# A gated delta net's preparation and recurrence emitted with a scheduling priority 300 places over the projection beside them

## The chip, the core and the metric

The kernel runs on one core of a Trainium2 chip. Its engines are named as in the profile: PE is TensorE (PEld is its loading of weights), DVE is VectorE, ACT is ScalarE, POOL is GpSimd and SP is SyncE, which here only issues DMAs. Each engine works through a queue of its own in order, and waits at an instruction whose inputs or buffers another engine has not yet finished. The metric is the device time of one execution in microseconds; the kernel before takes 3442.72 us, the median of 3 runs (3442.59 to 3445.05).

## The reference

A streaming encoder of four layers: gated delta net, mLSTM, gated delta net, mLSTM, each followed by a convolutional feed-forward layer, over 16 learned tokens and 1024 frames of 1024 features. DEPTH is 2, so the kernel has one delta net and one mLSTM. Only the delta net is touched by the change. Its reference, cut to what matters (16 value heads, 8 query and key heads, head size 128):

```python
proj = h @ w_in
qkv = silu(causal_depthwise_conv(proj[..., :o1], conv_w))     # 4 taps
z = proj[..., o1:o2]                                          # the gate of the output
beta = sigmoid(proj[..., o2:o3])
g = -exp(a_log) * softplus(proj[..., o3:] + dt_bias)
q, k = l2_normalize(q), l2_normalize(k)                       # one q, k for two value heads
G = cumsum(g within a chunk)
decay = exp(G_i - G_j) where i >= j else 0
a_mat = eye + (k*beta) @ k.T * decay * strictly_lower
u, w = triangular_solve(a_mat, [v*beta, k*beta*exp(G)])
attn = q @ k.T * decay;  qd = q * exp(G);  kt = k * exp(G_last - G)
# over the chunks, state S:
v_new = u - w @ S
o = qd @ S + attn @ v_new
S = S * exp(G_last) + kt.T @ v_new
out = (rms_norm(o, norm_w) * silu(z)) @ w_out
```

## The kernel before

The 1044 used positions (16 + 1024, and four of padding) are cut into 3 blocks of 348, and the delta net works in chunks of 116, so three chunks to a block. Features lie across the 128 partitions. One query and key head with its two value heads, in one block, is a step n: 8 heads times 3 blocks are 24 steps, and head h has the steps 3h to 3h + 2. The profile shows the stage of these steps from 82.9 us to about 1140 us.

**The projection** of a head is six tiles of 128 features (`gi`): q, k, two of v and two gate tiles. A tile and a block are 24 matmuls of 128x348 into one PSUM bank `pj_gi` (L233 to L235, because a float32 product is made of three products of a rounded part `wh`, `xh` and a rest `wl`, `xl`). L308 (`take`) then reads the bank on DVE; for q, k and v the four convolution taps follow (one on ACT at L695, three on DVE at L697). The weights come by DMA into 9 raw buffers; ACT casts them (L137) and POOL subtracts (L138) into 10 split buffers, a tile ahead. While the delta net works on head h, the second half of its own gates and the first four tiles of head h + 1 are projected, two tiles beside each step. After the two tiles, **the silu burst** runs on ACT over their six pages (L724): a table load, six activations and a load of the table with exp and ln (L727). It already has a priority of 100000 and the order within it is fixed.

**The preparation** of a step (`gdn_prepare`) normalises k, computes the masked products kk and qk of k and q in each chunk (L576, L579), and then does for each of the two value heads (`decay_block`, then the first part of `inverse`): three transposes spread the decay over a bank `row` (L559); ACT makes `eG` of it (L561); DVE makes `E` (L566), and ACT its exponential (L567); DVE multiplies kk by E into `ah` and masks it to `l` (L911, L912); POOL makes `A` from the same (L914), its rest `al`, and the products `att` (L764) and `qd` (L767). eG, E and A share three buffers:

```python
eG = self.core.tile([P, BS], F32, tag="e", name=f"eG_{name}", bufs=3)   # L560
E = self.core.tile([CH, BS], F32, tag="e", name=f"E_{name}", bufs=3)    # L562
A = self.core.tile([CH, BS], F32, tag="e", name=f"A_{name}", bufs=3)    # L913
```

so that the second head's E has to wait until one of the first head's is no longer read. Then the triangular matrix is inverted (`inverse`): Z is l plus the identity (L920, DVE), the first matmul transposes it (L923), and six levels follow, each with three matmuls in turn (L949, L958 and a third) and an operation of DVE or ACT behind each (`pl` at L953, `X`, `Z`), all in float16; a correction step ends it. The inverses of the two value heads are advanced in turn. The matmuls of the projection fill TensorE's time while such a chain waits for DVE and ACT.

**The recurrence** of a step (`gdn_recur`) goes through three chunks: transposes of k and v (`tr`, L795; `vt` on ACT, `ktb` on DVE at L797), the product with the state (`ks`, L828), the solution (`w`, `wv`), the state's update (`S` at L848; `St` on DVE at L854, two a chunk), and the outputs. **The finish** (`gdn_finish`) normalises and gates the output of the step before (L262, L265 are the square root's ln and exp; `osq`, `gy`) and stores it.

**What sets the order.** Python generators are emitted in turn by `weave`, in proportion to the numbers beside them: in a step n the preparation of n + 1 (27 parts), the recurrence of n (14), the finish of n - 1 (4) and the projection (8), or for the last three steps the output projection (28). Every instruction gets a place by this order of emission. A scheduler then writes each engine's queue: among the instructions of an engine whose inputs its own timing model holds ready, the one with the smallest place goes next. `tc.high_priority(n)` makes it count as n places earlier. That is in use already at three places: the readers of PSUM banks (`take`, `combine`) and the accumulators have 300, and the silu burst 100000. PSUM has two banks each for the projection (`pj`), for all products of the preparation, recurrence and finish (`sp`), and for the inverse (`pp`, `px`).

Of the kernel before, what the change touches and what calls it, by code (L numbers as in the profile page):

```python
# [64 lines left out]
def weave(*parts):  # L65

    live = [[g, max(n, 1), 0] for g, n in parts]
    while live:
        p = min(live, key=lambda p: (p[2] + 0.5) / p[1])
        try:  # L70
            next(p[0])
            p[2] += 1
        except StopIteration:
            live.remove(p)


def run(g):
    for _ in g:
        pass


class Trunk:
# [185 lines left out]
    def over_features(self, ps, acc, name):  # L268

        nc = self.nc  # L270
        hi, lo = [self.page("part", f"{z}_{name}", 2, F32R)[:, : acc.shape[1]] for z in ("ah", "al")]
        nc.scalar.copy(hi, acc)
        nc.vector.tensor_tensor(lo, acc, hi.bitcast(F32), ALU.subtract)
        nc.tensor.matmul(ps, self.ones, hi, start=True, stop=False)
        nc.tensor.matmul(ps, self.ones, lo, start=False, stop=True)

    def const(self, v):
        return self.consts[v]
# [327 lines left out]
    def gdn(self):  # L606
        a = self.a
        self.o_dram = [self.pd.tile([P, 2, TP], F32, tag=f"o_g_{h}", name=f"o_g_{h}", bufs=1) for h in range(NQK)]
        self.pages_of = {}
        self.blocks = {}  # L610
        n_all = NQK * NB
        tiles = lambda h: [h, NQK + h, 2 * NQK + 2 * h, 2 * NQK + 2 * h + 1, 32 + 2 * h, 32 + 2 * h + 1]

        def silu(h, tiles):
            self.burst([y for i in tiles for y in self.pages_of[h, i]], self.last, AF.Silu)

        def project(n):


            h, part = divmod(n, NB)  # L620
            i = (4, 0, 2)[part]
            g = h + (part > 0)
            yield from self.gdn_project(g, tiles(g)[i : i + 2], i)
            silu(g, (i, i + 1))

        def enter(b):
            hs = []
            for m in range(KD):
                h = self.page("C", f"hs_in_{b}_{m}", N_PAGES)
                sl = slice(b * BS, (b + 1) * BS)  # L630
                nc.sync.dma_start(h, self.hs[:, m, sl])
                self.put_input(h, m, sl)
                hs.append(h)
            return hs

        nc = self.nc
        t0 = tiles(0)
        weights = lambda t: self.split_weights(a["gdn_w_in"][t], f"gi{t}")
        self.new_input(0, "in")
        self.rt = self.new_factors("in")  # L640
        wg = self.split_weights(a["gdn_gate_w"], "gdn_gates", 32)
        hs = [enter(0)]
        ws = [weights(t0[0])]
        self.tables()
        hs.append(enter(1))
        ws.append(weights(t0[1]))
        hs.append(enter(2))
        rows = []
        for b in range(NB):
            acc = self.squares(hs[b], f"in{b}")  # L650
            self.now.append(lambda acc=acc, b=b: self.norm(acc, f"in{b}", self.r(b)))
            rows.append(self.gate_rows(wg, b, "gdn"))
            if b == NB - 1:
                gates = self.gdn_gates(rows)
                next(gates)
            for i in range(2):
                run(self.gdn_unit(0, i, t0[i], ws[i], b))
        lb, tb = next(gates)
        silu(0, (0, 1))
        order = t0[2:4] + [t for h in range(NQK) for t in tiles(h)[4:] + (tiles(h + 1)[:4] if h + 1 < NQK else [])]  # L660
        self.queue_weights([(a["gdn_w_in"][t], f"gi{t}") for t in order], 1)

        def first():
            yield from self.gdn_project(0, tiles(0)[2:4], 2)
            silu(0, (2, 3))

        weave((self.gdn_prepare(0, tb, lb), 13), (first(), 6))
        out = self.out_projection(a["gdn_w_out"], NQK, "go", GDN_CORE, GDN_LATE, 1, 2)
        for n in range(n_all):
            parts = [(self.gdn_recur(n, tb), 14)]  # L670
            if n + 1 < n_all:
                parts.insert(0, (self.gdn_prepare(n + 1, tb, lb), 27))
            if n:
                parts.append((self.gdn_finish(n - 1), 4))
            parts.append((project(n), 8) if n <= n_all - NB else (islice(out, 28), 28))
            weave(*parts)
        weave((self.gdn_finish(n_all - 1), 4), (out, 30))
# [620 lines left out]
    def ffn(self, L, order, row, post, pre):  # L1298
# [19 lines left out]
        for t, g in seq:  # L1318
            run(group(t, g))
            if (t, g) == (1, 1) and pre is not None:  # L1320
                self.new_input(pre, name)
                for part in [z for p in self.xt for z in p]:
                    nc.gpsimd.memset(part[:, NTOK:].bitcast(F32), 0.0)
                for m in range(KD):
                    h = self.raw_input(f"hi_{name}_{m}").rearrange("p n c -> p (n c)")
                    nc.sync.dma_start(h, self.new_hs[:, m, :HB])
                    self.put_input(h, m, slice(0, HB))
# [54 lines left out]
    def ffn_phase(self, L, row, post, pre):  # L1382
        self.wide = True
        self.ffn_constants(L)
        order = self.ffn_plan(L)
        run(self.out)
        self.ffn(L, order, row, post, pre)
# [110 lines left out]
```

## Time and profile before

| | us |
|---|---|
| median of 3 runs | 3442.72 |
| the profiled execution | 3444.23 |
| its span in the trace | 3442.5 |
| up to the first prepared block (0 to 82.9) | 82.9 |
| the steps of the delta net (82.9 to 1113.4) | 1030.5 |
| the last blocks and the start of the output projection (1113.4 to 1240) | 126.6 |
| the rest: feed-forward and mLSTM layers (1240 to 3442.5) | 2202.5 |

Instructions stand in the profile with the line, the operation, the tile they write and those they read, their shape, how often (x), and behind the bar the busy time, the mean of one in ns, and the idle time of the engine before them. An item of the timeline has its start in us, its duration, and in brackets how long its engine waited ahead of it and for what. A row of the waits has the total in us, the count and the longest. Matmuls are pipelined, so that their durations overlap, and the start of the next one tells more than the end. The granted clock is 0.969 on average. The projection's matmuls are the largest group of the delta net on TensorE; the first of its three products:

```profile
L233 PE MATMUL pj_gi<-xh_in,wh_gi 128*128 128x348 f32 x1152 | 394.2, 342 | 5.5 <-ACT wh_gi L137 3.7
```

### The profile page before, as it was taken

The page shows a single profiled execution, that of the slowest core. Times are in us where ns is not written, and L with a number is a line of the kernel's source. Part 1 is how long each engine was busy: PE and PEld are TensorE (multiplying, and loading weights), DVE is VectorE, ACT ScalarE, POOL GpSimd, SP SyncE. Part 2 cuts the span into 40 slices and gives each one's busy share as a digit, 9 for nine tenths or more (in the row PEclk, how much of TensorE's full clock was granted, in tenths as well). Part 3 has the DMA queues.
Part 4 walks back from the last instruction along what each step waited for, and adds up shares of the span by engine and source line. Part 5 has one row for each costly group of instructions (what it writes and reads, how often), then busy time and mean ns, then how long its engine had stood idle before and what let it go on. Part 6 is the DMA issues. An engine that isn't in the chain of part 4 may idle for free. (4 is left out here: it accounts for less than half of the span.)

```text
span 3442.5 us, 68429 instructions
## 1 busy us (share of the span) xinstructions
PE 3212.2 (93%) x25368; PEld 3119.6 (91%) x25368; DVE 2373.1 (69%) x5143; ACT 1609.0 (47%) x3390; POOL 1652.2 (48%) x1890
## 2 busy tenths in 40 slices
PE   7999999999999998799999989899998799999998
PEld 6889988988988897799999989899998799999998
DVE  7777777777767649877677484534469867777474
ACT  5455545555545435655455243323345645445232
POOL 2433443444334444577665434333344477666453
PEclk9999999999999999899999999999999899999999
DMA  3011100101001344422224453211125422224452
GB/s 118 23 37 34 34 29 31 34 32 34 31 31 40 107 132 152 134 93 93 78 78 133 133 182 125 93 44 50 56 78 183 136 90 87 87 75 132 132 180 88
DMA packets 234511, 297.75 MB, mean 86 GB/s; under 512 B 20684, under 2 KB 167104, under 8 KB 234176
## 3 DMA queue, kind: packets, MB, share of 16 engines
q1 hardware_dynamic: 234176, 293.37, 26.3%
q8 instruction: 200, 3.28, 0.4%
q14 instruction: 135, 1.11, 0.1%
HBM read 240.06 MB, written 53.23 MB: 85 GB/s over the span
## 5 line engine op out<-in xcount | busy, mean ns | idle before, releaser
L233 PE MATMUL pj_gi<-xh_in,wh_gi 128*128 128x348 f32 x1152 | 394.2, 342 | 5.5 <-ACT wh_gi L137 3.7
L233 PE MATMUL dn_f<-so_f,wh_f 128*128 128x260 f32 x1344 | 386.6, 288 | 11.8 <-ACT wh_f L137 5.0
L235 PE MATMUL pj_gi<-xh_in,wl_gi 128*128 128x348 f32 x1152 | 395.7, 343 | 0.9 <-POOL wl_gi L138 0.9
L234 PE MATMUL pj_gi<-xl_in,wh_gi 128*128 128x348 f32 x1152 | 393.5, 342 | 0.0
L235 PE MATMUL dn_f<-so_f,wl_f 128*128 128x260 f32 x1344 | 384.7, 286 | 0.0
L234 PE MATMUL dn_f<-so_f,wh_f 128*128 128x260 f32 x1344 | 384.5, 286 | 0.0
L138 POOL TENSOR_TENSOR wl_f<-wr_f,wh_f 128x512 fp32r<-128x512 f32 x168 | 226.0, 1362 | 246.0 <-ACT wh_f L137 113.5
L1278 DVE SCALAR_TENSOR_TENSOR z<-u,fcw,z 128x260 f32<-128x260 f32 x528 | 243.4, 487 | 49.8 <-ACT z L1276 35.0
L138 POOL TENSOR_TENSOR wl_u_s<-wr_u,wh_u_s 128x512 fp32r<-128x512 f32 x176 | 228.2, 1300 | 97.7 <-ACT wh_u_s L137 97.3
L233 PEld LDWEIGHTS dn_f<-so_f,wh_f 128*128 128x128 f32 x1344 | 257.7, 192 | 13.6 <-ACT z L1276 5.5
L441 DVE TENSOR_TENSOR acc_f<-acc_f,dn_f 128x260 f32<-128x260 f32 x320 | 133.1, 421 | 189.2 <-PE dn_f L235 188.2
L234 PEld LDWEIGHTS dn_f<-so_f,wh_f 128*128 128x128 f32 x1344 | 258.2, 192 | 0.2
L235 PEld LDWEIGHTS dn_f<-so_f,wl_f 128*128 128x128 f32 x1344 | 258.2, 192 | 0.1
L1276 ACT ACTIVATE z<-u,fcb,fcw 128x260 f32<-128x260 f32 x352 | 192.3, 570 | 93.7 <-DVE u L196 92.4
L233 PEld LDWEIGHTS pj_gi<-xh_in,wh_gi 128*128 128x128 f32 x1152 | 222.1, 193 | 8.0 <-ACT wh_gi L137 4.0
L235 PEld LDWEIGHTS pj_gi<-xh_in,wl_gi 128*128 128x128 f32 x1152 | 222.6, 193 | 2.4 <-POOL wl_gi L138 1.2
L234 PEld LDWEIGHTS pj_gi<-xl_in,wh_gi 128*128 128x128 f32 x1152 | 222.2, 193 | 0.7 <-issue 0.2
L138 POOL TENSOR_TENSOR wl_gi<-wr_gi,wh_gi 128x512 fp32r<-128x512 f32 x96 | 132.4, 1380 | 157.8 <-ACT wh_gi L137 153.8
L137 ACT CAST wh_u_s<-wr_u 128x512 fp32r<-128x512 f32 x176 | 105.9, 615 | 192.5 <-PE up L234 134.9
L697 DVE SCALAR_TENSOR_TENSOR gy<-u_g,c_gdn_conv_w_g,gy 128x348 f32<-128x348 f32 x288 | 187.9, 663 | 7.9 <-ACT gy L695 5.4
L138 POOL TENSOR_TENSOR wl_u_a<-wr_u,wh_u_a 128x512 fp32r<-128x512 f32 x132 | 170.1, 1293 | 37.0 <-ACT wh_u_a L137 36.3
L137 ACT CAST wh_f<-wr_f 128x512 fp32r<-128x512 f32 x168 | 103.1, 617 | 178.8 <-PE dn_f L234 133.0
(501 smaller groups left out, 11718.0 us busy)
## 6 DMA issues: line engine op xcount, KB each, us to landing
wr_u<-in_ffn_w_up_dram SPq DMA_DIRECT2D x224, 256.0 KB, 2.6
wr_f<-in_ffn_w_down_dram SPq DMA_DIRECT2D x176, 256.0 KB, 2.8
wr_gi<-in_gdn_w_in_dram SPq DMA_DIRECT2D x96, 256.0 KB, 2.6
h<-y SPq DMA_DIRECT2D x176, 130.0 KB, 2.3
si_f<-h SPq DMA_DIRECT2D x88, 260.0 KB, 3.5
wr_go<-in_gdn_w_out_dram SPq DMA_DIRECT2D x64, 256.0 KB, 2.7
wr_mi<-in_ml_w_in_dram SPq DMA_DIRECT2D x44, 256.0 KB, 2.6
o_g<-gy SPq DMA_DIRECT2D x48, 174.0 KB, 1.8
```

Source lines behind the costliest of these rows:

```text
L137: nc.scalar.copy(hi, part(raw))
L138: nc.gpsimd.tensor_tensor(lo, part(raw), hi.bitcast(F32), ALU.subtract)
L233: nc.tensor.matmul(out, w[0], x[0], start=start, stop=False)
L234: nc.tensor.matmul(out, w[0], x[1], start=False, stop=False)
L235: nc.tensor.matmul(out, w[1], x[0], start=False, stop=stop)
L441: nc.vector.tensor_tensor(acc[m][n], acc[m][n], ps, ALU.add)
L697: ins = nc.vector.scalar_tensor_tensor(y, u[:, j : j + BS], taps[:, j : j + 1], y, ALU.mult, ALU.add)
L1276: nc.scalar.activation(z, p[:, 2 : 2 + QB], AF.Identity, scale=taps[:, 2:3], bias=self.fcb[:, tt : tt + 1])
L1278: nc.vector.scalar_tensor_tensor(z if i or not h else y[h], p[:, i : i + QB], taps[:, i : i + 1], z, ALU.mult, ALU.add)
```

## The change

The steps of `gdn_recur` and `gdn_prepare` in the loop over n are each emitted within `high_priority(300)`, and so count as 300 places earlier than the projection and the finish that are emitted beside them. The preparation of the first step, ahead of the loop, is as it was.

```diff
+CHAIN = 300
 
+    def in_front(self, g):
+
+        while True:
+            with self.tc.high_priority(CHAIN):
+                if next(g, g) is g:
+                    return
+            yield
 
         for n in range(n_all):
-            parts = [(self.gdn_recur(n, tb), 14)]
+            parts = [(self.in_front(self.gdn_recur(n, tb)), 14)]
             if n + 1 < n_all:
-                parts.insert(0, (self.gdn_prepare(n + 1, tb, lb), 27))
+                parts.insert(0, (self.in_front(self.gdn_prepare(n + 1, tb, lb)), 27))
             if n:
                 parts.append((self.gdn_finish(n - 1), 4))
             parts.append((project(n), 8) if n <= n_all - NB else (islice(out, 28), 28))
             weave(*parts)
```

The instructions are the same; their order in the queues of PE, DVE and ACT changes from the first steps of the delta net up to the end of its last block, and is the same before and behind. The changed file has four more lines ahead of the class and eight more from `in_front` on, so that a line such as L559 is L571 in it, and L234 is L238.

In DVE's queue, at the entrance of the inverse in block 0 of a head (the head of 619.9 to 756.3 us), before; `l_8_0` and `l_9_0` are the masked matrices (the buffers of `l0`) of the block's two value heads, `E_0_8398` the second head's E:

```order
L566 TENSOR_SCALAR E_0_8398<-row_0_8392,dt_s_gdn,gd_lb 116x116 x3
L797 TENSOR_TENSOR ktb_2_1_8420<-tr_2_1_8422,dt_kt_gdn 116x256
L920 TENSOR_TENSOR Z_0_8451<-l_8_0_8382,i_162 116x348
L911 TENSOR_TENSOR ah_0_8403<-scs_kk_0_8327,E_0_8398 116x348
L308 TENSOR_TENSOR u_g_0_8863<-pj_gi_0_8779,r_in 128x348
L912 TENSOR_TENSOR l_9_0_8405<-ah_0_8403,c_m_g 116x348
L953 TENSOR_TENSOR pl_0_2_8470<-pp_0_2_8466,c_mlev_g 116x174
L920 TENSOR_TENSOR Z_0_8459<-l_9_0_8405,i_162 116x348
```

And after:

```order
L578 TENSOR_SCALAR E_0_8398<-row_0_8392,dt_s_gdn,gd_lb 116x116 x3
L809 TENSOR_TENSOR ktb_2_1_8420<-tr_2_1_8422,dt_kt_gdn 116x256
L924 TENSOR_TENSOR l_8_0_8382<-ah_0_8380,c_m_g 116x348
L923 TENSOR_TENSOR ah_0_8403<-scs_kk_0_8327,E_0_8398 116x348
L932 TENSOR_TENSOR Z_0_8451<-l_8_0_8382,i_162 116x348
L924 TENSOR_TENSOR l_9_0_8405<-ah_0_8403,c_m_g 116x348
L866 SCALAR_TENSOR_TENSOR St_2_0_8481<-St_1_2_8080,dt_gt_gdn,S_2_0_8478 128x128 x2
L932 TENSOR_TENSOR Z_0_8459<-l_9_0_8405,i_162 116x348
```

The first head's mask `l_8_0` has moved from ahead of the second E to behind it, Z has moved from ahead of the second head's `ah` to behind it, and the projection's `u_g` has left this place.

In TensorE's queue, in block 2 of the same head, before; `pj_gi_1_9763` is a bank of the next projection, and the last matmul of the gate projection's bank `pj_gi_2_9536` stands 48 instructions ahead of the first of these rows:

```order
L576 MATMUL sc_kk_2_9592<-gy_2_8286 116x116 x3
L576 MATMUL sc_qk_2_9623<-gy_2_8059,gy_2_8286 116x116 x3
L233 MATMUL pj_gi_1_9763<-xh_in_105,wh_gi_1_9408 128x348
L828 MATMUL ks_1_0_9629<-St_0_2_9335,gy_1_8251 116x256
L234 MATMUL pj_gi_1_9763<-xl_in_106,wh_gi_1_9408 128x348
L235 MATMUL pj_gi_1_9763<-xh_in_105,wl_gi_1_9409 128x348
L233 MATMUL pj_gi_1_9763<-xh_in_107,wh_gi_1_9408 128x348
L559 MATMUL row_2_9638<-c_ident_g,dt_G_gdn 128x116 x3
```

And after, from the last two matmuls of the gate projection on:

```order
L238 MATMUL pj_gi_2_9536<-xl_in_108,wh_gi_1_8995 128x348
L239 MATMUL pj_gi_2_9536<-xh_in_107,wl_gi_1_8996 128x348
L237 MATMUL pj_gi_0_9610<-xh_in_93,wh_gi_0_9404 128x348
L238 MATMUL pj_gi_0_9610<-xl_in_94,wh_gi_0_9404 128x348
L588 MATMUL sc_kk_2_9592<-gy_2_8286 116x116 x3
L588 MATMUL sc_qk_2_9623<-gy_2_8059,gy_2_8286 116x116 x3
L239 MATMUL pj_gi_0_9610<-xh_in_93,wl_gi_0_9405 128x348
L840 MATMUL ks_1_0_9629<-St_0_2_9335,gy_1_8251 116x256
L237 MATMUL pj_gi_0_9610<-xh_in_95,wh_gi_0_9404 128x348
L571 MATMUL row_2_9638<-c_ident_g,dt_G_gdn 128x116 x3
```

Between the gate projection's last matmul and `row` stood 46 of the next projection's matmuls; now four stand there, and kk, qk and `row` follow the gate projection closely.

In ACT's queue at the same place, before; `rs_k` is of the preparation's norm, `gy_2_9561` the last page of the silu burst over the gate projection, and `eG_2_9642` reads the `row_2_9638` of the rows above:

```order
L724 ACTIVATE gy_2_9561<-gy_2_9561 128x348
L727 ACT_TABLE_LOAD
L262 ACTIVATE rs_k_2_9579<-kn_2_9572,cvals 128x348
L796 COPY vt_1_0_9585<-tr_1_0_9586 116x256
L265 ACTIVATE rs_k_2_9579<-rs_k_2_9579 128x348
L695 ACTIVATE gy_0_9709<-u_g_0_9710,c_gdn_conv_w_g 128x348
L272 CAST ah_o_0_9803<-osq_0_0_9635 128x348
L561 ACTIVATE eG_2_9642<-row_2_9638 128x348
L695 ACTIVATE gy_1_9859<-u_g_1_9860,c_gdn_conv_w_g 128x348
L567 ACTIVATE E_2_9644<-E_2_9644 116x348
```

And after:

```order
L736 ACTIVATE gy_1_9534<-gy_1_9534 128x348
L736 ACTIVATE gy_2_9561<-gy_2_9561 128x348
L739 ACT_TABLE_LOAD
L573 ACTIVATE eG_2_9642<-row_2_9638 128x348
L579 ACTIVATE E_2_9644<-E_2_9644 116x348
L573 ACTIVATE eG_2_9665<-row_2_9661 128x348
L707 ACTIVATE gy_0_9709<-u_g_0_9710,c_gdn_conv_w_g 128x348
```

The norm's two operations and the copy `vt` have moved ahead of the burst, and eG now stands directly behind the burst's second table load.

## The prediction

> **What bounds the kernel now.** I read the page first, then the busy times by stretch, then the waits of TensorE in one head.
>
> ```profile
> PE 3212.2 (93%) x25368; PEld 3119.6 (91%) x25368; DVE 2373.1 (69%) x5143; ACT 1609.0 (47%) x3390; POOL 1652.2 (48%) x1890
> ```
> ```profile
> 82.90:1113.40 1030.50, 968.52 (x8086) 922.45 (x8086) 774.65 (x1849) 525.59 (x1181) 409.86 (x500) 0.98 0.10 32
> 619.90:756.30 136.40, 128.65 (x1081) 122.47 (x1081) 103.56 (x248) 71.06 (x160) 54.97 (x69) 0.99 0.10 32
> ```
>
> The columns of the two stretches are length, then busy time of PE, PEld, DVE, ACT and POOL, granted clock, DMA share and GB/s. The first is the delta net from its first prepared block to its last projection: TensorE idles 62.0 us of 1030.5, and DMA is no limit (0.10). The second is one head, three blocks: 136.4 us, 7.75 of them idle. So TensorE is the bound, and the most that a better order could win here is about 62 us, 1.8% of the kernel. The heads repeat, so I work on this one head (blocks 0, 1 and 2) and multiply by 8. TensorE's two largest waits there of four (total us, count, longest), and two of the three kinds of matmul that make up the inverse's levels, over the first 1240 us:
>
> ```profile
> PE px L923 <- DVE Z L920: 5.6, 5, 1.5
> PE S L848 <- DVE E L566: 1.5, 2, 0.9
> ...
> ```
> ```profile
> L949 PE MATMUL pp<-X,ah 116*116 116x64 f16 (+2 forms) x864 | 91.8, 217 | 0.0
> L958 PE MATMUL px<-pl,Z 116*116 116x64 f16 (+2 forms) x864 | 88.2, 212 | 0.0
> ```
>
> The reader sees that 7.1 of the 7.75 us are lost at the entrance of the inverse: at its first matmul (L923, which needs Z) and at the state matmul beside it. The levels that follow (L949, L958) show 0.0 of idle time before them in the whole stage. **So this change is decided at the entrance.** There the chain in block 0 is:
>
> ```profile
> 625.76 0.51 PE L559 MATMUL row<-c_ident_g,dt_G_gdn 116*128 116x116 f32 x3 [0.23 <-DVE scs_qk L579]
> 626.31 0.46 ACT L561 ACTIVATE eG<-row 128x348 f32<-128x348 f32 x1 [1.11 <-PE row L559]
> 628.42 1.61 POOL L914 TENSOR_TENSOR A<-scs_kk,E 116x348 f32<-116x348 f32 x1 [0.64 <-ACT E L567]
> 629.99 1.03 POOL L764 TENSOR_TENSOR att<-scs_qk,E 116x348 f32<-116x348 f32 x1
> 631.05 1.01 DVE L566 TENSOR_SCALAR E<-row,dt_s_gdn,gd_lb 116x116 f32<-116x116 f32 x3 [0.83 <-POOL att L764]
> 631.98 0.41 DVE L797 TENSOR_TENSOR ktb<-tr,dt_kt_gdn 116x256 f32<-116x256 f32 x1
> 632.32 0.63 DVE L920 TENSOR_TENSOR Z<-l,i 116x348 f16<-116x348 f16 x1
> 632.86 1.25 DVE L911 TENSOR_TENSOR ah<-scs_kk,E 116x348 f16<-116x348 f32 x1
> 634.04 0.51 DVE L308 TENSOR_TENSOR u_g<-pj_gi,r_in 128x348 f32<-128x348 f32 x1
> 634.47 0.65 DVE L912 TENSOR_TENSOR l<-ah,c_m_g 116x348 f16<-116x348 f16 x1
> 635.03 0.33 DVE L953 TENSOR_TENSOR pl<-pp,c_mlev_g 116x174 f16<-116x174 f32 x1
> 635.28 0.73 DVE L920 TENSOR_TENSOR Z<-l,i 116x348 f16<-116x348 f16 x1
> 635.93 0.59 DVE L854 SCALAR_TENSOR_TENSOR St<-St,dt_gt_gdn,S 128x128 f32<-128x128 f32 x2
> 636.07 0.37 PE L923 MATMUL px<-i,Z 116*116 116x116 f16 x3 [0.99 <-DVE Z L920]
> ```
>
> From the row matmul to the second inverse's L923 are 10.31 us. The second E comes 5.29 us after the row matmul; 2.6 of them are GpSimd's A and att, which give its buffer back only when att ends (631.02). A scheduling priority changes none of these durations, only how many projection matmuls lie beside them and what stands ahead of them in a queue. Blocks 1 and 2, from row to second L923:
>
> ```profile
> 669.54 0.51 PE L559 MATMUL row<-c_ident_g,dt_G_gdn 116*128 116x116 f32 x3
> 680.01 0.37 PE L923 MATMUL px<-i,Z 116*116 116x116 f16 x3 [0.49 <-DVE Z L920]
> 709.71 0.46 PE L559 MATMUL row<-c_ident_g,dt_G_gdn 116*128 116x116 f32 x3
> 721.51 0.37 PE L923 MATMUL px<-i,Z 116*116 116x116 f16 x3 [1.24 <-DVE Z L920]
> ```
>
> That is 10.47 and 11.80 us.
>
> **Term 1: the filler at the entrance.** The price of a projection matmul:
>
> ```profile
> 622.89 0.87 PE L576 MATMUL sc_kk<-gy 128*116 128x116 f32 x6
> 624.13 0.41 PE L234 MATMUL pj_gi<-xl_in,wh_gi 128*128 128x348 f32 x1
> 624.38 0.69 PE L828 MATMUL ks<-St,gy 128*116 128x256 f32 x2
> 624.71 0.51 PE L235 MATMUL pj_gi<-xh_in,wl_gi 128*128 128x348 f32 x1
> 625.06 0.32 PE L233 MATMUL pj_gi<-xh_in,wh_gi 128*128 128x348 f32 x1
> 625.21 0.32 PE L234 MATMUL pj_gi<-xl_in,wh_gi 128*128 128x348 f32 x1
> ```
>
> Durations overlap, so starts count: 0.15 to 0.16 us for a projection matmul behind another (625.06 to 625.21), 0.25 behind a chain matmul (624.13 to 624.38), so a change from chain to projection costs about 0.09. Between the row matmul and the second L923 the order has 35, 33 and 37 projection and finish matmuls now, and 30, 29 and 47 after the change. With 0.16 each, six or seven changes (0.5), and the chain's own matmuls there (about 1.6 to 2.2 us), the filler is 7.8, 8.1 and 8.0 us now, and 7.4, 7.2 and 10.1 then. What the chain needs beyond its filler is stall: now 2.5 + 2.3 + 3.8 = 8.6 us a head (the wait view shows a little less, since it counts from modelled ends).
>
> **Term 2: DVE's queue at the entrance.** Block 0's queue after the second E becomes ktb, l, ah, Z, l, two St, Z, where it was ktb, Z, ah, u_g, l, pl, Z. By start-to-start times: 0.34 + 0.56 + 1.18 + 0.54 + 0.56 + 0.59 + 0.65 = 4.42 against 3.95 us (the St pair by its 0.59). The first l moved from the shadow of the wait at 631.05 to behind it. So 10.31 becomes 10.8, and the stall 3.4 (from 2.5). In block 1 an l comes behind the wait (0.6) and a wv and a pl leave (0.34, 0.25): still 10.5, with 7.2 of filler a stall of 3.3 (from 2.3).
>
> **Term 3: block 2 runs into the silu burst.** Block 2's filler grows by ten matmuls, which alone would end its stall. But the row matmul now stands 18 matmuls behind the last one of the gate projection (4 projection, 12 kk and qk, 2 ks: about 1.0 + 1.24 + 0.33, 2.5 us), and its eG stands on ScalarE directly behind the silu burst over that projection. Now there are 10 us between them. The burst:
>
> ```profile
> 699.76 0.62 ACT L137 CAST wh_gi<-wr_gi 128x512 fp32r<-128x512 f32 x1 [0.95 <-PE pj_gi L234]
> 700.40 1.28 ACT L724 ACT_TABLE_LOAD   x1
> 701.69 2.41 ACT L724 ACTIVATE gy<-gy 128x348 f32<-128x348 f32 x6
> 704.12 1.28 ACT L727 ACT_TABLE_LOAD   x1
> 705.42 0.55 ACT L262 ACTIVATE rs_k<-kn,cvals 128x348 f32<-128x348 f32 x1
> ```
>
> The weight cast ahead of the burst waits for the last matmuls of that projection, so the next operation of ScalarE comes 5.7 us after it (699.76 to 705.42), about 5.8 after the projection's end. eG, 0.5 us behind its row matmul now, would then be 5.8 - 2.5 = 3.3 us behind it: 2.9 later. The latency is 10.8 + 2.9 = 13.7 us against 10.1 of filler: stall 3.6 (from 3.8). What is queued behind eG on ScalarE is E, the second eG and a convolution tap; DVE's E and through it TensorE wait for them. Bounds: no delay, if the burst could start earlier (stall 0.5 or less), and the whole 5.7 (stall 6.4). I take 2.9, since the cast's wait is in the row.
>
> [...]
>
> **Term 4: the rest.** Changes from chain to projection fall from 88 to 82 a head: -0.5 us. The levels get denser (54, 42, 53 projection matmuls between first L923 and last inverse matmul become 42, 38, 41), and they have no wait that could be won, so their cost is 0 or more. If two taps of 0.5 us a block came ahead of a level it would be 3 us a head; DVE's share of these stretches stays near 85% by the counts, so I take 0.5. The last block, where the out-projection is the filler:
>
> ```profile
> 1126.41 0.81 PE L559 MATMUL row<-c_ident_g,dt_G_gdn 116*128 116x116 f32 x3
> 1139.76 0.37 PE L923 MATMUL px<-i,Z 116*116 116x116 f16 x3 [2.25 <-DVE Z L920]
> ```
>
> 13.35 us for 9.2 of filler now; then 5.2 of filler for 10.8 to 13.35: the stall of 4.1 becomes 5.6 to 8.1. I take +2.5, later waits of the shorter tail included. Weight loads, POOL's splits and the DMA queue keep their order within a few places and their lead of a tile: nothing.
>
> **Sum.** A head: +0.9 + 1.0 - 0.2 - 0.5 + 0.5 = +1.7 us; eight heads, the first with more room, about +12.5; tail +2.5: **+15 us**. The profiled execution took 3444.2 us (span 3442.5), 1.5 above the median of 3442.7; on the median that is **3457**.
>
> **The rivals.**
> *Block 2's filler pays (faster).* If eG is not held by the burst, the stalls are 2.9 + 3.3 + 0.2 instead of 8.6, with the changes -2.7 a head: 3421 us. For it: the filler count is sure. Against it: the cast's wait and one queue on ScalarE. Chance 0.20.
> *DVE's f16 operations stop being stretched.* One L911 takes 1.25 us beside GpSimd's work, another much less:
>
> ```profile
> 628.71 0.51 DVE L911 TENSOR_TENSOR ah<-scs_kk,E 116x348 f16<-116x348 f32 x1
> ```
>
> If GpSimd's new order freed the second ah of each block, 0.7 us go three times a head: -17, to 3440. [...] Against it: al, qd and A stay beside that ah in the new order. Chance 0.08.
> *It cancels:* the delay of eG is half of 2.9 and the gains of term 4 offset blocks 0 and 1: 3443. Chance 0.14.
> *The denser levels stall too:* 3 us a head instead of 0.5: 3477. Chance 0.12.
> *The chain is not moved:* the order shows it moved in every block; no chance. The forecast keeps 0.46.
>
> **How the numbers follow.** Faster by over 0.2% (6.9 us, about what a measurement here can tell): 0.20; within: 0.08 + 0.14 = 0.22; slower: 0.46 + 0.12 = 0.58. The forecast alone spans 3450 to 3466; the range reaches to the dense levels above and near the faster rival below: 3424 to 3478.
>
> **What would show it.** Right: waits at L923 of blocks 0 and 1 grow by about 1 us, eG of block 2 starts right after the second table load, some 3 us behind its row matmul, L949 and L958 stay near zero. Wrong: a head shorter than 136 us, or a block 2 whose eG follows its row by 0.5 us.

## The result, and the profile after

The changed kernel takes 3493.9 us (median of 4 runs, 3492.35 to 3496.4) against 3443.89 us before: 1.0135 times as long (95% interval 1.0103 to 1.0166), 50 us slower. The forecast was 3457 with a range up to 3478: the sign was right, the size was not. The profile's first lines, for the engine that bounds, and two stretches: the steps from the first prepared block to the last projection, and the same head as before, block by block the same instructions (columns as before):

```profile
span 3492.2 us, 68538 instructions
PE 3254.4 (93%) x25368; PEld 3154.7 (90%) x25368; DVE 2391.6 (68%) x5143; ACT 1606.6 (46%) x3390; POOL 1659.0 (48%) x1890
```
```profile
82.90:1154.50 1071.60, 1000.99 (x8088) 948.74 (x8087) 792.49 (x1849) 523.89 (x1184) 417.21 (x500) 0.95 0.09 30
636.40:779.80 143.40, 134.24 (x1081) 127.33 (x1080) 105.73 (x248) 70.67 (x160) 56.31 (x69) 0.95 0.09 31
```

TensorE has as many matmuls as before (25368) and is busy for 42.2 us more; its idle time, span less busy time, grew by only 7.5 us (230.3 to 237.8). In the head it idles 9.2 us instead of 7.75, but the head is 7.0 us longer. The granted clock tells the two apart: 0.95 in the head where it was 0.99. TensorE's waits in this head, in full (total us, count, longest):

```profile
PE w L851 <- DVE r L844: 2.5, 1, 2.5
PE sc_kk L588 <- DVE gy L762: 2.1, 1, 2.1
PE sc_qk L588 <- DVE scs_kk L591: 1.2, 1, 1.2
PE S L860 <- DVE E L578: 1.1, 1, 1.1
PE ks L840 <- DVE St L866: 0.8, 2, 0.4
PE px L935 <- DVE Z L932: 0.7, 1, 0.7
PE ks L840 <- DVE scs_kk L591: 0.6, 1, 0.6
```

The wait at the inverse's first matmul (now L935), 5.6 us in five pieces before, is down to 0.7. In its place stand two long waits that were not there: the recurrence's `w` for `r`, and `kk` for the norm of k. From 82.9 to 1240 us these three are as follows, where before the inverse's was 46.5 us and those at `w` and `kk` 0.6 and 1.1:

```profile
PE w L851 <- DVE r L844: 20.8, 12, 2.5
PE sc_kk L588 <- DVE gy L762: 13.1, 11, 2.5
PE px L935 <- DVE Z L932: 9.9, 12, 1.6
```

The first, in block 1 of the head, on TensorE, DVE and GpSimd:

```profile
692.42 0.32 PE L238 MATMUL pj_gi<-xl_in,wh_gi 128*128 128x348 f32 x1
695.23 0.45 PE L851 MATMUL w<-r,XT 116*116 116x128 f32 x2 [2.49 <-DVE r L844]
```
```profile
692.98 1.01 DVE L578 TENSOR_SCALAR E<-row,dt_s_gdn,gd_lb 116x116 f32<-116x116 f32 x3 [1.72 <-POOL att L776]
693.90 0.92 DVE L924 TENSOR_TENSOR l<-ah,c_m_g 116x348 f16<-116x348 f16 x1
694.74 0.34 DVE L844 SCALAR_TENSOR_TENSOR r<-ks,dt_nE_gdn,vt 116x128 f32<-116x128 f32 x1
```
```profile
689.59 1.29 POOL L142 TENSOR_TENSOR wl_gi<-wr_gi,wh_gi 128x512 fp32r<-128x512 f32 x1 [0.67 <-ACT wh_gi L141]
690.84 1.21 POOL L926 TENSOR_TENSOR A<-scs_kk,E 116x348 f32<-116x348 f32 x1
692.01 0.94 POOL L776 TENSOR_TENSOR att<-scs_qk,E 116x348 f32<-116x348 f32 x1
```

`r` stands in DVE's queue behind the second head's E and a mask, and that E waits for GpSimd to end `att` (692.01 + 0.94 is 692.95), which frees its buffer. The second wait, in block 2: the chain from `kn` through ACT to k's multiplication takes 6.9 us (720.96 to 727.88), longer than the matmuls beside it:

```profile
720.96 0.35 PE L278 MATMUL kn<-ah_k,ones 128*128 128x348 f32 x1
725.06 0.55 ACT L266 ACTIVATE rs_k<-kn,cvals 128x348 f32<-128x348 f32 x1
726.01 0.49 ACT L269 ACTIVATE rs_k<-rs_k 128x348 f32<-128x348 f32 x1
726.53 1.29 DVE L762 TENSOR_TENSOR gy<-gy,rs_k 128x348 f32<-128x348 f32 x1 [0.83 <-ACT rs_k L269]
727.88 0.86 PE L588 MATMUL sc_kk<-gy 128*116 128x116 f32 x6 [2.10 <-DVE gy L762]
```

In TensorE's order, 14, 39 and 42 projection matmuls stood between `kn` and `kk` in the three blocks of a head before, and 16, 14 and 16 now. What the wait at `w` does to the clock, in four stretches from 3.4 us ahead of it:

```profile
688.96:692.37 3.41, 3.41 (x23) 3.16 (x22) 1.96 (x3) 1.29 (x3) 2.78 (x3) 1.00 0.26 74
692.38:695.79 3.41, 0.92 (x6) 0.46 (x4) 2.81 (x7) 0.49 (x1) 3.29 (x5) 1.00 0.14 54
695.79:709.44 13.65, 13.57 (x74) 12.49 (x74) 7.61 (x21) 3.47 (x9) 1.70 (x2) 0.50 0.00 1
709.44:719.68 10.24, 10.24 (x118) 10.05 (x117) 7.44 (x22) 5.57 (x16) 2.13 (x3) 1.00 0.05 17
```

The reader sees a window of 3.41 us in which TensorE was busy for 0.92, then 13.65 us at half clock though TensorE has no wait: 74 matmuls, 5.4 a microsecond, against 11.5 in the stretch behind. Half of 13.65 is 6.8 us, where the head before lost half of a single window (1.7 us); with the 1.4 us of further idle time that is 6.5 of the 7.0 us by which the head is longer. Over the whole kernel the record of the granted clock lists stretches at half clock of 280.8 us, 215.1 before, all but the last (which ends with the kernel) in multiples of 3.41 us; between 100 and 1215 us they are 119.5 and 51.2 us. There, 11 stretches make up the 119.5 us. The window ahead of each tells where it comes from: in eight of them (88.7 us) its longest wait is that at `w`, in one (23.9 us, in the last block) a wait of 2.0 us at the state's matmul, and in two (3.4 us each) the wait at `kk`.

So each span can be taken apart into three: TensorE's **idle time**; the **loss by the clock**, half of its busy time in the stretches at half clock; and the rest, its **work** at full clock. Before: 230.3 + 84.8 + 3127.4. After: 237.8 + 119.5 + 3134.9. Of the 49.7 us, the clock has 34.7, the waits 7.5 and the work 7.5. Half is a little too much: projection matmuls that follow each other start 292 ns apart in stretches at half clock and 160 outside them (medians over all traces), so that a busy microsecond there loses 0.45; by that estimate the clock has 31 us. The levels of the inverse look busier too, while the mean of one has grown by 4 or 5 ns only:

```profile
L961 PE MATMUL pp<-X,ah 116*116 116x64 f16 (+2 forms) x864 | 113.2, 221 | 0.5 <-ACT X L936 0.5
L970 PE MATMUL px<-pl,Z 116*116 116x64 f16 (+2 forms) x864 | 94.6, 217 | 0.0
```

For the second row the clock explains it: one of its matmuls takes up 159 ns of TensorE in a stretch at half clock and 102 outside, about as before (99). The first row's matmuls also stand further apart at full clock (124 ns each, 104 before), because the order is another. This raises a rival, the **levels theory**: the inverse's levels stand denser, hold each other up unseen within the modelled ends of the matmuls, and the low clock is only a mark. The **clock theory** is that a wait that fills most of a window halves the clock for the windows behind it.

### The profile page after: what moved, and what is told of

It reads as the page before. It is cut to its first block, busy times and chain, and to the rows that moved or that the text cites. A ratio compares the mean times of both kernels' runs of the same rounds, so it can differ in the third digit from the quotient of the medians.

```text
span 3492.2 us, 68538 instructions
## 1 busy us (share of the span) xinstructions
PE 3254.4 (93%) x25368; PEld 3154.7 (90%) x25368; DVE 2391.6 (68%) x5143; ACT 1606.6 (46%) x3390; POOL 1659.0 (48%) x1890
## 5 line engine op out<-in xcount | busy, mean ns | idle before, releaser
L238 PE MATMUL pj_gi<-xl_in,wh_gi 128*128 128x348 f32 x1152 | 396.0, 344 | 0.0
L238 PE MATMUL dn_f<-so_f,wh_f 128*128 128x260 f32 x1344 | 382.8, 285 | 0.0
L238 PEld LDWEIGHTS dn_f<-so_f,wh_f 128*128 128x128 f32 x1344 | 256.8, 191 | 0.2
L238 PEld LDWEIGHTS pj_gi<-xl_in,wh_gi 128*128 128x128 f32 x1152 | 223.9, 194 | 0.5
L709 DVE SCALAR_TENSOR_TENSOR gy<-u_g,c_gdn_conv_w_g,gy 128x348 f32<-128x348 f32 x288 | 200.0, 701 | 17.7 <-ACT gy L707 15.7
```

The costliest lines, as they stand in the source:

```text
L238: nc.tensor.matmul(out, w[0], x[1], start=False, stop=False)
L709: ins = nc.vector.scalar_tensor_tensor(y, u[:, j : j + BS], taps[:, j : j + 1], y, ALU.mult, ALU.add)
```

## The experiments

The last three columns come from the trace of each run's profiled execution, which in some differs from the median by up to 23 us. Most of that spread is the clock's as well: the four executions of prep_only have spans from 3529.7 to 3567.2 us, while span times granted clock is 3358.6 to 3365.0; for the five of late1_before it is 3456.6 to 3480.1 against 3330.5 to 3337.3. Ratios are to the kernel before, run on the same chip.

| kernel | median us | ratio (95%) | span | idle | clock | work |
|---|---|---|---|---|---|---|
| before | | | 3442.5 | 230.3 | 84.8 | 3127.4 |
| changed | 3493.9 | 1.0135 (1.0103 to 1.0166) | 3492.2 | 237.8 | 119.5 | 3134.9 |
| late1_before | 3463.6 | 1.0061 (1.0035 to 1.0086) | 3480.1 | 230.8 | 126.6 | 3122.7 |
| late2_before | 3460.8 | 1.0040 (1.0022 to 1.0059) | 3467.2 | 237.3 | 103.6 | 3126.3 |
| prep_only | 3546.2 | 1.0287 (1.0257 to 1.0316) | 3567.2 | 254.9 | 183.6 | 3128.6 |
| recur_only | 3434.0 | 0.9974 (0.9964 to 0.9984) | 3430.4 | 219.4 | 73.2 | 3137.8 |
| kn_back | 3453.7 | 1.0032 (1.0019 to 1.0045) | 3452.3 | 240.3 | 77.9 | 3134.1 |
| chain100 | 3484.6 | 1.0123 (1.0108 to 1.0139) | 3480.4 | 244.9 | 103.4 | 3132.1 |
| four_e_after | 3514.3 | 1.0209 (1.0179 to 1.0239) | 3528.2 | 244.3 | 148.7 | 3135.1 |
| four_e_before | 3423.6 | 0.9938 (0.9916 to 0.9960) | 3418.3 | 211.9 | 71.5 | 3134.9 |
| four_e_recur | 3428.0 | 0.9950 (0.9931 to 0.9970) | 3432.4 | 209.6 | 80.8 | 3142.1 |
| fill20_after | 3491.3 | 1.0133 (1.0113 to 1.0153) | 3487.0 | 246.4 | 87.8 | 3152.8 |
| fill_ks | 3494.8 | 1.0143 (1.0119 to 1.0167) | 3492.9 | 248.1 | 93.6 | 3151.1 |

**The wait alone, with the order untouched.** In the kernel before, `att` of the first value head is computed once or twice more in block 1 of each head, so that the second E's buffer comes free 1.03 or 2.06 us later. The orders of TensorE, DVE and ACT stay word for word those of before.

```diff
             nc.gpsimd.tensor_tensor(att, qk, E, ALU.mult)
+            if i == 0 and b == 1:
+                for _ in range(2):
+                    nc.gpsimd.tensor_tensor(att, qk, E, ALU.mult)
```

With two more:

> The kernel before, whose order on TensorE stays as it is, with att of the first value head computed three times in block 1 of each head, so that its buffer and with it the second E come 2.06 us later on 8 occasions. Clock theory: where the longer wait passes about 2.4 us in one piece the clock falls, so up to 16.5 us of wait and 8 times 3.4 to 6.8 us of half clock: 3475 to 3510. Levels theory: the wait alone, 3459 at most.

With one more (`range(1)`):

> The kernel before with att of the first value head computed twice instead of three times in block 1 of each head: half the delay (1.03 us) of the run with three, which gave +17 us in the median and +25 in its profiled execution, 19 of them by the clock. Clock theory: idle time +3 to 4 us, and as many low windows as waits pass half of a 3.4 us window: 3447 to 3460, work at full clock 3127 as before. Waits alone: 3445 to 3449.

The run with one more settles most. Its first lines, and its largest group of waits (46.5 us in 40 pieces before, in the same window):

```profile
span 3480.1 us, 68437 instructions
PE 3249.3 (93%) x25368; PEld 3156.8 (91%) x25368; DVE 2371.9 (68%) x5143; ACT 1609.0 (46%) x3390; POOL 1659.3 (48%) x1898
```
```profile
PE px L926 <- DVE Z L923: 48.8, 33, 2.8
```

Idle time and work are those of before (+0.5 and -4.7 us), the instructions on TensorE and their order too, and yet this execution is 37.6 us longer, because TensorE is busy for 37.1 us more. The clock's 41.8 us make that up; with 0.45 in place of the half it is 37.8, and the work of the three kernels with one order on TensorE (before, late1_before, late2_before) is then 3135.6, 3134.9 and 3136.3 us. The profiled execution is the slowest of its five; at the median the run is 19 us slower than before, where waits alone were to cost 5 at most. No rearrangement of levels can be behind it, since there is none: the levels theory, by which the low clock is only a mark, falls. What changed is the length of single waits: at the inverse's entrance nine of them are longer than 2 us, where two were before, although their sum grew by 2.3 us only. In this kernel 14 of the 16 stretches at half clock between 100 and 1215 us follow a window whose longest wait is there. The two runs also show what neither theory had in its numbers: half the delay costs no less than the whole (3463.6 and 3460.8 us). So what counted in these two runs was not how long TensorE waited in sum, but how long single waits were; that it also counts how they lie to the windows is the author's reading, which no run tried by itself. The clock theory's expectation for one more delay missed by 4 us, that for two by 14, on the other side; the latter run lies close to what waits alone were to give (3459 at most), and by itself would not tell the theories apart.

**One part of the change alone.** First the preparation in front, and the recurrence at its own place:

```diff
-            parts = [(self.in_front(self.gdn_recur(n, tb)), 14)]
+            parts = [(self.gdn_recur(n, tb), 14)]
```

> Only the preparation is in front, the recurrence has its own place. Its order on TensorE leaves 13, 15 and 40 projection matmuls between the norm of k (kn) and kk in the blocks 0, 1 and 2 (14, 42, 39 before; 16, 14, 16 in the changed kernel), and 15 between ks and w (8 before, 11 changed). Clock theory (a 3.4 us window that TensorE spends idle by half or more is followed by half clock): one of the two long waits, that for k's norm, stays in one block a head, the one for r goes; 3465 (3450 to 3480), and the sum idle + half of the busy time at low clock + 3130 gives the span within 12 us. Levels theory: the inverse is as dense as in the changed kernel, 3485 to 3495.

It was 102 us slower than before, far outside what was expected: the clock's loss is 98.8 us more, with seven stretches of 20 to 24 us at half clock in the stage. The wait that the changed kernel had lost at the inverse's entrance is back, in pieces of up to 3.0 us:

```profile
PE px L935 <- DVE Z L932: 43.9, 27, 3.0
```

Then the recurrence in front, and the preparation at its own place:

```diff
-                parts.insert(0, (self.in_front(self.gdn_prepare(n + 1, tb, lb)), 27))
+                parts.insert(0, (self.gdn_prepare(n + 1, tb, lb), 27))
```

> Only the recurrence is in front. TensorE's order has 16, 19 and 45 projection matmuls between kn and kk, and 7 between ks and w. Clock theory: waits at kk in blocks 0 and 1 and at w behind the second E remain in part, 3460 (3445 to 3480), and the sum idle + half of the busy time at low clock + 3130 gives the span within 12 us. Levels theory: the inverse has its own places, so no loss, 3440 to 3448.

It was 10 us faster than before, better than either expectation. Its waits are many and short, the longest of the two largest groups 2.7 and 1.0 us:

```profile
PE px L935 <- DVE Z L932: 16.5, 26, 2.7
PE S L860 <- DVE E L578: 13.2, 14, 1.0
```

Between 100 and 1215 us it has 6.8 us at half clock, in one piece. So of the two parts it is the preparation that costs, and the recurrence's priority takes about half of that back: +102 alone, +50 with it. The changed kernel with k's norm, kk and qk back at their places (`in_front` skips the first three parts of the preparation):

```diff
-        while True:
-            with self.tc.high_priority(CHAIN):
+        for i in count():
+            with self.tc.high_priority(1 if i in skip else CHAIN):
```

> The changed kernel with k's norm, kk and qk back at their own places; the rest of the preparation (decay, inverse) and the recurrence stay in front. 16, 19 and 45 projection matmuls between kn and kk. Clock theory: the waits at kk fall by about half, those at w stay: 3475 (3460 to 3490), by the same sum. Levels theory: 3485 to 3495, since the inverse stays in front.

3453.7 us: 40 of the 50 us go with it, and its clock loss is below that of before (77.9 against 84.8), while it idles 10 us more than before. So the early norm, kk and qk are the dear part of the preparation when the recurrence is in front too. Both theories missed: that of the levels expected 3485 or more, with the inverse still in front, and that of the clock 3460 or more. The wait at `kk` falls to 5.9 us, but that is not where the gain comes from, since in the changed kernel only two short stretches at half clock follow it. The longest wait at `w` falls from 2.5 to 1.8 us, and the seven stretches behind waits for `r` there last one window each, where the eight of the changed kernel last 11 us on average. Why they are shorter, no run shows.

**A smaller priority.**

```diff
-CHAIN = 300
+CHAIN = 100
```

> The changed kernel with 100 places instead of 300. The counts around kk (16, 14, 15) and w (7) are those of 300 or less, so the same waits: 3485 (3470 to 3500) in both theories; by the clock theory the time follows the number of low windows.

As expected by both theories: 3484.6 us. The 300 places are not what decides; 100 move the same chains.

**The buffer that the second E waits for.** A fourth buffer for eG, E and A (`bufs=4` at their four places, and five instead of six for the convolution's tails to make room), in the changed kernel:

```diff
-        E = self.core.tile([CH, BS], F32, tag="e", name=f"E_{name}", bufs=3)
+        E = self.core.tile([CH, BS], F32, tag="e", name=f"E_{name}", bufs=4)
```

> The changed kernel with four buffers instead of three for eG, E and A (and one less for the convolution's tails, to make room), so that the second E no longer waits for GpSimd's att and r not for E. Clock theory: the 2.49 us wait at w goes and with it the low clock in seven heads: 3450 (3435 to 3465). Levels theory: only waits at the entrance go, at most 10 to 15 us: 3480 to 3490.

A clear miss: 20 us slower than the changed kernel. The wait at `w` did shrink, from 20.8 to 8.8 us, but the waits at the entrance came to 30.6 us and one at `kk` to 3.1 us, and the loss by the clock rose by 29.2 us. A wait taken away at one place moved the others. In the kernel before:

> The kernel before with the same fourth buffer. Both theories: the 46.5 us that the first matmul of the inverse waits for Z shrink by about half; the clock theory adds the few low stretches of the stage (some 44 us at half clock, 22 us). Clock theory: 3410 (3400 to 3425). Levels theory: 3420 (3415 to 3430).

3423.6 us, the fastest of the study and 0.6% ahead of the kernel before; the gain is 18.4 us of idle time and 13.3 of clock, against 7.5 of work. It was expected at 3410 by the clock theory and 3420 by the other, so it does not tell them apart. With the recurrence in front as well:

> The recurrence alone in front, with the fourth buffer for eG, E and A. Recurrence alone gave 3434, the fourth buffer alone 3424. Clock theory: both take waits away at the entrance, partly the same ones, and leave hardly a low window in the stage: 3413 (3405 to 3424). Levels theory has no view of its own: 3410 to 3425.

3428.0 us: the two gains do not add up.

**Filling the wait.** Twenty matmuls without use stand in front of `w` in block 0's chunk 1 of each head, so that TensorE works through the wait for `r` (the lines that tie them behind `r`, and `w` behind them, are not shown):

```diff
+            for j in range(20 if prev is not None else 0):
+                with self.tc.high_priority(100000):
+                    fill = nc.tensor.matmul(pw[:, 2 * P :], self.ones, self.xt[j % KD][0][:, : 2 * P], start=True, stop=True)
+                self.order(fill, prev)
+                prev = fill
```

> The changed kernel plus 20 matmuls without use (the rounded projection input times ones, 128x256, into the unused half of the bank of w) directly ahead of the recurrence's w matmul of chunk 1 in block 0 of each head, where TensorE now waits 2.49 us for DVE's r. The wait for r stays; TensorE works through it. Clock theory (a wait that leaves TensorE idle for most of a 3.4 us window halves its clock for the 13.7 us behind it, 6.8 us a head, and that is about 36 of the 50 us): the low clock behind this wait goes, the time falls by 30 to 48 us, to 3446 to 3464. Levels theory (the loss is in the inverse's denser levels, and the low clock is only a mark of waits): no gain, the same 3494 or up to 15 us slower.

The time did not fall as expected (3491.3 us). The clock did come back, 31.7 us of loss less than in the changed kernel, but the matmuls did not lie in the wait: they waited themselves, 12.8 us in eight pieces, until a DVE operation on E had released them (their bank of `w` is one of the two that the rows behind E use too), and so they added 17.9 us of work, while idle time rose by 8.6. The same with the bank of `ks`, which is held already:

> As the run that filled the wait at w with 20 matmuls without use, but these go into the unused half of the bank of ks, which TensorE already holds, so that they need not wait for a bank. Clock theory: low windows of the heads mostly go (-30 us), the 20 matmuls cost 17 us of work and take some 10 of waiting away: 3460 to 3480. Levels theory: 3490 to 3510.

These waited for `r` themselves, behind a longer wait at the inverse's entrance:

```profile
696.10 0.37 PE L945 MATMUL px<-i,Z 116*116 116x116 f16 x3 [2.87 <-DVE Z L942]
697.53 3.87 PE L855 MATMUL ks<-xh_in,ones 128*128 128x256 f32 x20 [0.27 <-DVE r L844]
```

The loss by the clock is 25.9 us less, the work 16.2 more, and idle time 10.3 more, since the order around them moved: the waits at the entrance came to 43.8 us in 22 pieces. The sum is near zero again. The clock theory's expectation missed in both runs, and the times came out near those of the levels theory (the same 3494, and 3490 to 3510), though not by its reason, as the loss by the clock did fall. The two runs show the clock's share as an account, not as a gain, and neither filled the wait that it was made for. In the last, waits of 2.1 to 2.9 us were followed by a single window at half clock, 14 times; so the length of a wait did not set the length of the stretch behind it, which was 13.65 us behind the 2.49 us in the changed kernel.

## Why the prediction was wrong

**What bounds the kernel: right in part.** TensorE is the bound, and the waits at the entrance decide. But only idle time was weighed, as in the "about 62 us" that an order could win. The row that it quoted held the granted clock of 0.98 too, and over the whole kernel the loss by the clock was already a third as large as the idle time (84.8 against 230.3 us); the prediction did not ask what that clock cost or what sets it.

**Terms 1 and 2: right that the entrance changes, wrong on the direction.** Waits at the first matmul of the inverse were to grow by about 1 us a block; they fell from 46.5 to 9.9 us in all. From the first row matmul to the second inverse's first matmul:

```profile
642.23 0.46 PE L571 MATMUL row<-c_ident_g,dt_G_gdn 116*128 116x116 f32 x3
652.43 0.32 PE L935 MATMUL px<-i,Z 116*116 116x116 f16 x3
```
```profile
686.89 0.51 PE L571 MATMUL row<-c_ident_g,dt_G_gdn 116*128 116x116 f32 x3
698.63 0.55 PE L935 MATMUL px<-i,Z 116*116 116x116 f16 x3
```

Block 0 takes 10.20 us (10.8 foreseen). Block 1 takes 11.74 (10.5 foreseen), with the wait in it, and that wait is no longer at the inverse but at `w`, since `r` stands behind the E that waits for `att`. The prediction named that E's wait and DVE's queue behind it, but followed in the queue only the inverse's own operations.

**Term 3: right mechanism, half the size.** eG of block 2 starts directly behind the silu burst's second table load, as said, but 2.00 us behind its row matmul instead of 3.3, since the row matmul itself was held up by the wait at `kk`:

```profile
730.04 0.46 PE L571 MATMUL row<-c_ident_g,dt_G_gdn 116*128 116x116 f32 x3
...
741.00 0.32 PE L935 MATMUL px<-i,Z 116*116 116x116 f16 x3
```
```profile
727.02 1.28 ACT L736 ACT_TABLE_LOAD   x1
728.32 2.41 ACT L736 ACTIVATE gy<-gy 128x348 f32<-128x348 f32 x6
730.75 1.28 ACT L739 ACT_TABLE_LOAD   x1
732.04 0.46 ACT L573 ACTIVATE eG<-row 128x348 f32<-128x348 f32 x1
```

It costs nothing there: the block needs 10.96 us against 13.7 foreseen, and no wait is shown at its entrance. The 13.7 also started from block 0's 10.8, without a reason, where block 2 itself took 11.80 before. (The faster rival has a slip too: it counts block 0's stall as 2.9, against 3.4 in term 2; with 3.4 it comes to 3425, not 3421.) The first silu starts 1.30 us after the start of the load ahead of it (727.02 to 728.32), as it did before (1.29, 700.40 to 701.69).

**Left out: the wait at kk.** It is 13.1 us of the 76 that the view of waits lists from 82.9 to 1240 us, and the waits of qk behind it are 8.6. The prediction counted filler from the row matmul on; the 39 to 42 projection matmuls that covered k's norm were taken for work that could be moved for nothing.

**The sum, and the step that failed.** +15 us were forecast, of waits and denser levels. Idle time rose by 7.5 and the work by 7.5, together 15.0: right in sum, but by luck, since they come from other places than those named. The step that failed is the price of a wait, in the words of term 1 "What the chain needs beyond its filler is stall", with the stall then counted at its own length. In these traces half clock followed 349 of the 350 windows of 3.41 us in which TensorE was busy for a share of less than 0.44, and what the clock lost in this way beyond the loss of before is the 34.7 us that were missing. The forecast of levels that stay near zero held (0.5 and 0.0 us). So the rival of denser levels that stall has no support; late1_before shows besides that the clock's loss arises without denser levels. Nor does a run show the 0.7 us of the rival of stretched DVE operations as the price of GpSimd's work: before, the L911 that took 0.51 us (from 628.71) had GpSimd's A beside it too (628.42 to 630.03), and the mean of the 48 went from 0.89 us (42.62 in all) to 0.82 (39.43) in the changed kernel.

**What stays open.** How long a stretch at half clock will last, and whether a given wait falls into one window, could not be told beforehand from an order: of the eleven expectations by the clock theory two held in the median (chain100 and four_e_before). The account explains a time afterwards: where no matmuls were added the work is between 3123 and 3142 us, and in the three runs for which its sum was stated beforehand it came within 12 us of the span, as said there. It did not forecast the times. Denser levels may still make the stretches longer. Between 100 and 1215 us they last 3.2 windows on average in the changed kernel, 3.8 in prep_only and 3.9 in four_e_after, against 2.1 before and 2.3 in late1_before; but 1.2 in kn_back, where the inverse is in front too.

## What to carry to other kernels

Price a wait of the bounding engine by what it does to the granted clock, not by its length only: many waits of 1 us (recur_only, 73.2 us lost by the clock) were cheaper here than one of 2.5 us a head (the changed kernel, 119.5). Before moving a chain ahead of the work beside it, count that work for every link of the chain that waits, the first one too, and follow each operation that is queued behind a link that waits. Where parts of a change can be made alone, try each: here one part alone gains 10 us and the other loses 102.

## What was not expected of the hardware

Over the traces of all thirteen kernels, each window of 3.41 us at full clock was sorted by the share for which TensorE was busy, and by whether half clock followed:

| busy share of the window | followed by half clock | by full clock |
|---|---|---|
| under 0.44 | 349 | 1 |
| 0.44 to 0.50 | 177 | 53 |
| 0.50 to 0.60 | 29 | 130 |
| 0.60 and more | 1 | 11493 |

A busy share under 0.44, 1.9 us of waiting in one window, was followed by half clock in 349 of 350 cases, and the one exception lies at the border (0.4397). The shares are counted from ends of matmuls that the profile models. Nor did the full clock always come back after one busy window: stretches between 100 and 1215 us lasted for 3.4 to 23.9 us, although in 296 of their 301 windows TensorE was busy for 0.66 or more. The 126 windows that were the last of their stretch held a median of 4 matmuls of a projection and 6 in float16, the other 175 held 3 and 12. Whether the inverse's small matmuls, which are in float16, hold the clock down was not shown: no run tried it by itself.
